# Two residual blocks on one core: attention scores with their masks, and the value products of a head pair, issued as unbroken bundles

## The chip, the core and the metric

One core of a Trainium2 chip runs the whole kernel: TensorE (PE) multiplies matrices into PSUM, VectorE (DVE) and ScalarE (ACT) read PSUM and work in SBUF, GpSimd (POOL) does small pieces, SyncE (SP) issues the transfers. The metric is the device time of one execution in microseconds; lower is better.

## The reference

The input is 256 tokens of 1024 features. Four layers follow each other, each a mixer and a gated feed-forward net. The mixers, cut to what matters here:

```python
# layer 1: stick-breaking attention, 16 heads of 64
z = einsum('bhqd,bhkd->bhqk', q, k) * scale
log_1mb = where(s < t, log_sigmoid(-z), 0)
a = where(s < t, exp(log_sigmoid(z) + cumsum_after(log_1mb)), 0)
o = einsum('bhqk,bhkd->bhqd', a, v)
# layer 2: forgetting attention, 16 heads of 64
cum = cumsum(log_sigmoid(h @ w_fg + b_fg))          # per head and token
logits = where(s <= t, z + cum[t] - cum[s], -inf)
o = einsum('bhqk,bhkd->bhqd', softmax(logits), v)
# layer 3: differential attention, 8 heads with two maps each, over 256 tokens and 256 of a context
p = softmax(einsum("bqmhd,bkmhd->bmhqk", q, k) * scale)
o = einsum("bhqk,bkhd->bqhd", p[:, 0] - lam * p[:, 1], v)
# layer 4: a short convolution
```

Queries are handled in two blocks of 128, so the first block sees 128 keys and the second 256.

## The kernel before

The builder doesn't issue instructions. Each call such as `nc.tensor.matmul` is recorded (`record`) with what it depends on, and when the whole program is recorded, `schedule` makes one order: it walks through a planned time and gives each engine, whenever that engine is free in the plan, the ready operation that was recorded first and whose tiles fit in the buffers. `emit` then issues them in that order; the profile therefore names one line, L544, for nearly every instruction, and work is told apart by tile names. On the chip each engine runs its own list strictly in order.

Matrix products of weights are made in three parts (high times high, high times low, low times high; `mm3`) on float32r. Weights come in chunks of 1 MB (`w`); ScalarE rounds them to `wh` and VectorE takes the difference `wl`. VectorE also does the modulation vectors in the background (`w<-w,rows,vec`, results `raw` and `msh_*`).

In `attention1` (layers 1 and 2) a loop runs over the 8 head pairs: the projection products give `qkps`, copied to `qk`, which holds queries and keys of both heads of a pair, 64 rows each. `scores` makes one PSUM tile `z` per head with two regions: columns 0 to 128 for the first query block, 128 to 384 for the second. Each score product has 64 rows of weights and in float32 it runs as two instructions; the two heads of a pair lie in different halves of the array. Region by region it adds, in layer 2, the gates' sums (a product of a selector column `sel` with `hl`, made in `forget_cum`) and then the mask, a bfloat16 product of the unit matrix with the mask (`bf`). `weights_of` makes the weights `a` on ScalarE and VectorE, `transposed` turns them on TensorE (`atp`) and copies them (`at`), and the value products go to `op`: for each head a 256-column product and a 128-column one, 64 output rows each, so that the two heads again lie in different halves.

In `diff_attention` (layer 3) each of 16 units (head pair, query block, map) has six score products `dz` with 64 rows of weights, three for each head of the pair; then come the softmax (`dmx`, `p`), the transposes `dtp`, the value products `dop`, and the normed result `on`. Products of the values' projection (`acc`) stand between.

At a stage's end the last products go into `acc`; VectorE multiplies these with a gate (`u`), adds them to `x`, and ScalarE, GpSimd and VectorE make the next norm, for which TensorE makes the transposes `tps`.

Of the kernel before, what the change touches and what calls it, by code (L numbers as in the profile page):

```python
# [10 lines left out]
F32 = mybir.dt.float32  # L11
# [252 lines left out]
class Rec:  # L264
# [4 lines left out]
    def __init__(self):  # L269
        self.ops, self.limit, self.count, self.after = [], 0, 0, None  # L270

# [11 lines left out]

    def record(self, eng, fn, args, kw):
# [10 lines left out]
        if fn == "matmul" and not kw["start"]:  # L295
            ins.append(outs[0])
# [86 lines left out]
    def schedule(self, slots):  # L383
# [56 lines left out]
        left, low, far = len(ops), 0, []  # L440
        done = [False] * left
        while left:
# [21 lines left out]
            for e in engines:  # L464
                if engines[e] > now:
                    continue
                while ready[e]:
                    op = heapq.heappop(ready[e])[1]
                    lack = fits(op)
                    if lack is None:  # L470
                        best = op
                        break
                    blocked.setdefault(lack, []).append(op)
                if best:
                    break
# [3 lines left out]
            op = best  # L479
            for t in needs(op):  # L480
                free[t.cls] -= 1
                if t.group:
                    live[t.group] = live.get(t.group, 0) + 1
                t.real = True
                for o in blocked.pop(t.cls, ()):
                    heapq.heappush(pending[o.eng], (now, o.i, o))
# [96 lines left out]
class Builder:  # L583
# [443 lines left out]
    def forget_cum(self):  # L1027

        nc = self.nc
        hl = self.sb.tile([P, S], F32R, tag="hl", name="hl")  # L1030
        sel = self.sb.tile([P, 16], F32R, tag="sel", name="sel")
        nc.vector.tensor_copy(sel, self.cst[:, 256:272])
        zero = self.sb.tile([P, S], F32, tag="hf", name="zero")
# [29 lines left out]
        nc.vector.tensor_copy(hl[0:48], t["d"])  # L1063
        nc.vector.tensor_tensor(out=hl[32:48], in0=t["d"][32:48], in1=hl[32:48].bitcast(F32), op=ALU.subtract)
# [4 lines left out]
    def scores(self, j, qk, stick, cum):  # L1069
# [5 lines left out]
        for t, lo, hi in self.REGIONS:  # L1075
            for hh, z in enumerate(zs):
                rows = slice(64 * hh, 64 * hh + 64)
                q, k = qk[rows, t * P : (t + 1) * P], qk[rows, 256 : 256 + hi - lo]
                nc.tensor.matmul(z[:, lo:hi], lhsT=q, rhs=k, start=True, stop=False)
            for hh, z in enumerate(zs):  # L1080
                if cum is not None:
# [3 lines left out]
                        z[:, lo:hi], lhsT=sel[:, h : h + 1].to_broadcast([P, P]), rhs=hl[:, 0 : hi - lo], start=False,  # L1085
                        stop=False,
                    )
                nc.tensor.matmul(z[:, hi - P : hi], lhsT=self.eye_b, rhs=mask, start=False, stop=True)
# [43 lines left out]
    def attention1(self, i):  # L1132
# [13 lines left out]
        for it in range(KT + 2):  # L1146
# [17 lines left out]
            if 0 <= j < KT:  # L1164
# [3 lines left out]
                for hh in range(2):  # L1168
                    nc.tensor.matmul(
                        op[sl[hh], 0:256], lhsT=vs[0][:, cs[hh]], rhs=ats[hh][:, 0:256], start=True, stop=False  # L1170
                    )
                for hh in range(2):
                    nc.tensor.matmul(
                        op[sl[hh], 128:256], lhsT=vs[1][:, cs[hh]], rhs=ats[hh][:, 256:384], start=False, stop=True
                    )
# [171 lines left out]
    def diff_attention(self):  # L1347
# [67 lines left out]
        for it in range(U + VLAG + 3):  # L1415
# [3 lines left out]
            if it < U:  # L1419
                jp, t, m = it // 4, it % 4 // 2, it % 2  # L1420
                zs = [self.pmm.tile([P, 512], F32, tag="mm", name="dz") for hh in range(2)]
                for a, b in ((0, 0), (0, 1), (1, 0)):
                    for hh in range(2):
                        rows = slice(64 * hh, 64 * hh + 64)
                        nc.tensor.matmul(
                            zs[hh], lhsT=qT[m][a][rows, jp, t * P : (t + 1) * P], rhs=kT[m][jp // 2][b][rows, jp % 2, :],
                            start=a + b == 0, stop=a == 1,
                        )
# [226 lines left out]
```

## Time and profile before

| | |
|---|---|
| median of 3 runs | 1354.19 us (1352.99 to 1358.27) |
| the profiled execution's own time | 1356.83 us |
| its span in the profile | 1355.0 us |
| TensorE busy | 1318.0 us, 97% |
| VectorE busy | 1083.6 us, 80% |
| ScalarE busy | 716.2 us, 53% |
| granted TensorE clock, mean | 0.994 of full speed |

Span is the time from the first to the last instruction. Busy time is the union of an engine's instructions; products overlap in the pipeline, so for TensorE the distance from start to start says more than the length of one. The first attention's loop lies at about 60 to 150 us, the second's at 385 to 470, diff attention's scores at 756 to 846.

### The profile page before, as it was taken

To read this page: it belongs to the slowest core of one execution; us is meant where nothing else is said; L and a number is where in the kernel's file an instruction comes from. 1 tells how busy PE (TensorE), PEld (TensorE's weight loads), DVE (VectorE), ACT (ScalarE), POOL (GpSimd) and SP (SyncE) were. 2 spreads that over 40 slices of the span, in tenths; PEclk is the share of its full clock that TensorE was granted. 3 is DMA by queue.
4 is the path that set the end of the run, shared out by engine and by line. 5 is a ranking of instruction groups with operands and counts; after the bars stand their busy time and mean duration, and the time that the engine had idled before them with its cause. 6 is when DMAs were issued, how large, how long until landed. Compare 5 with 4: busy or idle time off the path is not lost.

```text
span 1355.0 us, 21985 instructions
## 1 busy us (share of the span) xinstructions
PE 1318.0 (97%) x8776; PEld 1178.4 (87%) x8776; DVE 1083.6 (80%) x1825; ACT 716.2 (53%) x1249; POOL 72.4 (5%) x102
## 2 busy tenths in 40 slices
PE   5999899999999999999999999899999999999998
PEld 3788799999898799999988777799999899899997
DVE  6888989899898499999799998886776898855542
ACT  3565655555656484556454567754444545744430
POOL 0000100000100000001033112100000000000000
PEclk9999999999999999999999999899999999999999
DMA  9857578887666256667544641576776688455520
GB/s 360 316 211 272 194 280 321 330 313 293 239 252 252 89 184 260 267 252 270 206 161 173 226 154 63 189 304 254 280 269 260 231 300 309 181 193 186 187 95 32
DMA packets 45320, 311.84 MB, mean 230 GB/s; under 512 B 5280, under 2 KB 5664, under 8 KB 8864
## 3 DMA queue, kind: packets, MB, share of 16 engines
q1 hardware_dynamic: 45216, 310.42, 61.3%
q8 instruction: 69, 1.13, 0.3%
q14 instruction: 35, 0.29, 0.1%
HBM read 309.35 MB, written 1.05 MB: 229 GB/s over the span
## 4 chain that ended last, share of the span: by engine, by line
PE 90%; DVE 6%; ACT 2%; issue 1%; DMA 0%; POOL 0%; SPq 0%; ACTq 0%; POOLq 0%
PE gu L544 34%; PE acc L544 30%; PE qkps L544 7%; PE fp L544 4%; PE cu L544 3%; PE z L544 2%; PE bb L544 2%; PE qps L544 2%; DVE w L544 2%; PE op L544 1%; DVE wl L544 1%; PE dop L544 1%; PE tps L544 1%; PE kc L544 1%; PE atp L544 1%
## 5 line engine op out<-in xcount | busy, mean ns | idle before, releaser
L544 DVE TENSOR_TENSOR wl<-w,wh 128x1024 fp32r<-128x1024 f32 x392 | 470.8, 1220 | 77.9 <-ACT wh L544 54.7
L544 ACT CAST wh<-w 128x1024 fp32r<-128x1024 f32 x392 | 402.4, 1049 | 98.8 <-DMA w<-in_wst_dram 56.7
L544 DVE CUSTOM_DVE_ANT_0 w<-w,rows,vec 128x1024 f32<-128x1024 f32 x192 | 242.4, 1278 | 9.9 <-DMA w<-in_wst_dram 9.6
L544 PE MATMUL gu<-h1h,wh 128*128 128x256 f32 x640 | 181.3, 283 | 0.0
L544 PE MATMUL gu<-h1h,wl 128*128 128x256 f32 x640 | 181.2, 283 | 0.0
L544 PE MATMUL gu<-h0h,wl 128*128 128x256 f32 x640 | 181.1, 283 | 0.0
L544 PE MATMUL gu<-h1l,wh 128*128 128x256 f32 x640 | 181.1, 283 | 0.0
L544 PE MATMUL gu<-h0l,wh 128*128 128x256 f32 x640 | 181.1, 283 | 0.0
L544 PE MATMUL gu<-h0h,wh 128*128 128x256 f32 x640 | 180.9, 283 | 0.0
L544 PE MATMUL acc<-wh,yh 128*128 128x512 f32 x352 | 137.6, 392 | 0.0
L544 PE MATMUL acc<-wl,yh 128*128 128x512 f32 x352 | 137.5, 391 | 0.0
L544 PE MATMUL acc<-wh,yl 128*128 128x512 f32 x352 | 135.3, 389 | 0.0
L544 PEld LDWEIGHTS gu<-h0l,wh 128*128 128x128 f32 x640 | 122.6, 192 | 2.2
L544 PEld LDWEIGHTS gu<-h0h,wh 128*128 128x128 f32 x640 | 122.5, 192 | 2.3
L544 PEld LDWEIGHTS gu<-h1l,wh 128*128 128x128 f32 x640 | 122.8, 192 | 0.1
L544 PEld LDWEIGHTS gu<-h1h,wh 128*128 128x128 f32 x640 | 122.8, 192 | 0.1
L544 PEld LDWEIGHTS gu<-h1h,wl 128*128 128x128 f32 x640 | 122.8, 192 | 0.0
L544 PEld LDWEIGHTS gu<-h0h,wl 128*128 128x128 f32 x640 | 122.6, 192 | 0.0
L544 DVE TENSOR_TENSOR y<-s,gu 128x256 f32<-128x256 f32 x80 | 33.5, 418 | 76.2 <-ACT s L544 76.2
L544 ACT ACTIVATE s<-gu 128x256 f32<-128x256 f32 x40 | 15.4, 385 | 138.0 <-PE gu L544 138.0
L544 PEld LDWEIGHTS acc<-wh,yl 128*128 128x128 f32 x352 | 66.1, 188 | 14.3
L544 PEld LDWEIGHTS acc<-wh,yh 128*128 128x128 f32 x352 | 66.3, 188 | 12.2 <-ACT yh L544 0.2
(364 smaller groups left out, 2690.4 us busy)
## 6 DMA issues: line engine op xcount, KB each, us to landing
w<-in_wst_dram SPq DMA_DIRECT2D x284, 1024.0 KB, 4.9
w<-in_wst_dram SPq DMA_DIRECT2D x16, 512.0 KB, 11.4
x<-in_x_dram SPq DMA_DIRECT2D x2, 512.0 KB, 6.6
cx<-in_ctx_dram SPq DMA_DIRECT2D x2, 512.0 KB, 6.3
out_dram<-x SPq DMA_DIRECT2D x1, 512.0 KB, 2.6
out_dram<-x SPq DMA_DIRECT2D x2, 256.0 KB, 2.0
cst<-in_consts_dram SPq DMA_DIRECT2D x1, 264.0 KB, 5.2
smalls<-in_smalls_dram SPq DMA_DIRECT2D x1, 256.0 KB, 5.2
```

Of the source, the lines that this page charges most:

```text
L544: fn(*[real(a) for a in op.args], **{k: real(v) for k, v in op.kw.items()})
```

## The change

It touches the recording layer and three places that use it.

- `together()` is new: operations recorded inside it form a bundle. The first operation takes over what the others wait for outside the bundle, and their tiles, and `schedule` lets the rest follow it on TensorE before anything else.
- `record` lets an accumulating product depend on its PSUM tile only where earlier writes overlap with it.
- `scores`: the score products of both regions come first (the wide region no longer opens with `start=True`), then, in layer 2, one product of 384 columns per head for the gates' sums in place of one of 128 and one of 256, then all masks.
- `forget_cum`: `hl` has 384 columns, the first 128 repeated, so two copies and two differences are made in place of one each; `hl` and the zero tile now need a slot of the next larger class.
- The four value products of a pair, and the six `dz` products of a unit, are bundles.

```diff
@@ class Rec
+    @contextmanager
+    def together(self):
+
+        n = len(self.ops)
+        yield
+        first, *rest = self.ops[n:]
+        inside = set(self.ops[n:])
+        for op in rest:
+            for d, kind in op.deps.items():
+                if d not in inside:
+                    first.deps.setdefault(d, kind)
+            op.deps.setdefault(first, 1)
+            for t in op.tiles:
+                if t not in first.tiles:
+                    first.tiles.append(t)
+                    t.ops.append(first)
+        self.follow[first] = rest
@@ def record
         if fn == "matmul" and not kw["start"]:
-            ins.append(outs[0])
+            v = outs[0]
+            if any(w[0] & v.mask and w[1] < v.parts[1] and w[2] > v.parts[0] for w in v.t.writes):
+                ins.append(v)
@@ def schedule
+                if e == "PE" and run:
+                    best = run.pop(0)
+                    taken.add(best)
+                    break
                 while ready[e]:
                     op = heapq.heappop(ready[e])[1]
+                    if op in taken:
+                        continue
...
             op = best
+            run += self.follow.get(op, ())
@@ def forget_cum
-        hl = self.sb.tile([P, S], F32R, tag="hl", name="hl")
+        hl = self.sb.tile([P, 384], F32R, tag="hl", name="hl")
...
-        nc.vector.tensor_copy(hl[0:48], t["d"])
-        nc.vector.tensor_tensor(out=hl[32:48], in0=t["d"][32:48], in1=hl[32:48].bitcast(F32), op=ALU.subtract)
+        for lo, n in ((0, P), (P, S)):
+            d, out = t["d"][:, 0:n], hl[:, lo : lo + n]
+            nc.vector.tensor_copy(out[0:48], d)
+            nc.vector.tensor_tensor(out=out[32:48], in0=d[32:48], in1=out[32:48].bitcast(F32), op=ALU.subtract)
@@ def scores
-        for t, lo, hi in self.REGIONS:
-            for hh, z in enumerate(zs):
-                rows = slice(64 * hh, 64 * hh + 64)
-                q, k = qk[rows, t * P : (t + 1) * P], qk[rows, 256 : 256 + hi - lo]
-                nc.tensor.matmul(z[:, lo:hi], lhsT=q, rhs=k, start=True, stop=False)
-            for hh, z in enumerate(zs):
-                if cum is not None:
+        with nc.together():
+            for t, lo, hi in self.REGIONS:
+                for hh, z in enumerate(zs):
+                    rows = slice(64 * hh, 64 * hh + 64)
+                    q, k = qk[rows, t * P : (t + 1) * P], qk[rows, 256 : 256 + hi - lo]
+
+                    nc.tensor.matmul(z[:, lo:hi], lhsT=q, rhs=k, start=t == 0, stop=False)
+            if cum is not None:
+                for hh, z in enumerate(zs):
                     hl, sel = cum
                     h = 2 * j + hh
                     nc.tensor.matmul(
-                        z[:, lo:hi], lhsT=sel[:, h : h + 1].to_broadcast([P, P]), rhs=hl[:, 0 : hi - lo], start=False,
-                        stop=False,
+                        z[:, 0:384], lhsT=sel[:, h : h + 1].to_broadcast([P, P]), rhs=hl, start=False, stop=False
                     )
-                nc.tensor.matmul(z[:, hi - P : hi], lhsT=self.eye_b, rhs=mask, start=False, stop=True)
+            for t, lo, hi in self.REGIONS:
+                for z in zs:
+                    nc.tensor.matmul(z[:, hi - P : hi], lhsT=self.eye_b, rhs=mask, start=False, stop=t == 1)
@@ def attention1, and in the same way the six products of diff_attention
+                with nc.together():
+                    for hh in range(2):
+                        nc.tensor.matmul(
+                            op[sl[hh], 0:256], lhsT=vs[0][:, cs[hh]], rhs=ats[hh][:, 0:256], start=True, stop=False
+                        )
```

What this makes of the order on TensorE is seen at three places; the other engines keep their instructions (VectorE has the two pieces more for `hl`), in an order that is partly changed inside the three attention stages on VectorE and ScalarE, and the order outside of these stages is the same. The first place is TensorE in the second attention's loop, the scores of one head pair (two tiles `z`, one per head; sizes are those of the output). Before:

```order
L544 MATMUL z_4661<-qk_4540 128x128
L544 MATMUL z_4667<-qk_4540 128x128
L544 MATMUL z_4661<-hl_3271,sel_3322 128x128
L544 LDWEIGHTS bf_429
L544 MATMUL z_4661<-bf_429 128x128
L544 MATMUL z_4667<-hl_3271,sel_3322 128x128
L544 LDWEIGHTS bf_429
L544 MATMUL z_4667<-bf_429 128x128
L544 MATMUL z_4661<-qk_4540 128x256
L544 MATMUL z_4667<-qk_4540 128x256
L544 MATMUL z_4661<-hl_3271,sel_3322 128x256
L544 LDWEIGHTS bf_429
```

After the change, the same pair:

```order
L573 MATMUL z_4639<-qk_4503 128x128
L573 MATMUL z_4640<-qk_4503 128x128
L573 MATMUL z_4639<-qk_4503 128x256
L573 MATMUL z_4640<-qk_4503 128x256
L573 MATMUL z_4639<-hl_3271,sel_3322 128x384
L573 MATMUL z_4640<-hl_3271,sel_3322 128x384
L573 LDWEIGHTS bf_429
L573 MATMUL z_4639<-bf_429 128x128
L573 LDWEIGHTS bf_429
L573 MATMUL z_4640<-bf_429 128x128
```

The wide region's score products have moved up behind the narrow ones, the four products for the gates' sums have become two, and the masks stand at the end, four in a row (two more rows of each follow). The second place is TensorE in the same loop, at the value products of the first head pair (`op`; `at` is one head's transposed weights). Before:

```order
L544 MATMUL op_4329<-at_4301,v_736_3897 64x256
L544 MATMUL qkps_4265<-h0h_3757,wh_4062 128x256
L544 MATMUL qkps_4265<-h0l_3767,wh_4062 128x256
L544 MATMUL qkps_4265<-h0h_3757,wl_4098 128x256
L544 MATMUL op_4329<-at_4326,v_736_3897 64x256
L544 MATMUL op_4329<-at_4301,v_737_3982 64x128
L544 MATMUL op_4329<-at_4326,v_737_3982 64x128
```

After the change:

```order
L573 MATMUL qkps_4354<-h0l_3767,wh_4222 128x256
L573 MATMUL op_4363<-at_4327,v_736_3897 64x256
L573 MATMUL op_4363<-at_4352,v_736_3897 64x256
L573 MATMUL op_4363<-at_4327,v_737_3982 64x128
L573 MATMUL op_4363<-at_4352,v_737_3982 64x128
L573 MATMUL qkps_4354<-h0h_3757,wl_4260 128x256
```

The three projection products no longer stand between the heads. In the order before, seven of the sixteen `op` units have other products between their heads, and one between its wide and its narrow products; after, none has. The third place is TensorE in diff attention, one of its last units (`dz`, one tile per head). Before:

```order
L544 MATMUL dz_9161<-kT01h_7784,qT0h_8169 128x512
L544 MATMUL dz_9161<-kT01l_7795,qT0h_8169 128x512
L544 MATMUL dz_9161<-kT01h_7784,qT0l_8187 128x512
L544 MATMUL acc_9084<-wl_8627,doh_8839 128x512
L544 MATMUL dz_9176<-kT01h_7784,qT0h_8169 128x512
L544 MATMUL dz_9176<-kT01l_7795,qT0h_8169 128x512
L544 MATMUL dz_9176<-kT01h_7784,qT0l_8187 128x512
```

After the change:

```order
L573 MATMUL dz_9219<-kT01h_7770,qT0h_8155 128x512
L573 MATMUL dz_9220<-kT01h_7770,qT0h_8155 128x512
L573 MATMUL dz_9219<-kT01l_7781,qT0h_8155 128x512
L573 MATMUL dz_9220<-kT01l_7781,qT0h_8155 128x512
L573 MATMUL dz_9219<-kT01h_7770,qT0l_8173 128x512
L573 MATMUL dz_9220<-kT01h_7770,qT0l_8173 128x512
```

The two heads' products alternate and nothing stands between; in the order before, six of the sixteen units are not in one alternating run.

## Rows read from the trace of the kernel before

**Rows 1.** Windows of the three attention stages; busy us (instructions) of each engine, clock, transfers.

```profile
63.00:136.00 73.00, 72.76 (x540) 58.96 (x539) 64.03 (x119) 42.38 (x79) 0.00 (x0) 1.00 0.67 254
385.00:456.00 71.00, 71.00 (x537) 59.33 (x535) 57.80 (x140) 39.57 (x98) 0.00 (x0) 1.00 0.65 237
756.00:860.00 104.00, 102.31 (x552) 75.68 (x551) 91.31 (x200) 74.64 (x163) 21.36 (x35) 1.00 0.40 146
```

**Rows 2.** Waits of TensorE over the span: total us, times, longest.

```profile
PE tps L544 <- DVE u L544: 4.8, 2, 3.0
...
PE dop L544 <- DVE on L544: 1.3, 3, 0.5
```

**Rows 3.** Timeline of TensorE, first attention: start us, length us, instruction.

```profile
63.02 0.28 PE L544 MATMUL qkps<-h1l,wh 128*128 128x256 f32 x1
63.14 0.28 PE L544 MATMUL qkps<-h1h,wl 128*128 128x256 f32 x1
63.35 0.49 PE L544 MATMUL z<-qk 64*128 64x128 f32 x4
63.77 0.28 PE L544 MATMUL z<-bf 128*128 128x128 bf16 x2
63.99 0.70 PE L544 MATMUL z<-qk 64*128 64x256 f32 x4
64.62 0.28 PE L544 MATMUL z<-bf 128*128 128x128 bf16 x2
```

**Rows 4.** Timeline of TensorE, one score unit of the second attention.

```profile
429.46 0.33 PE L544 MATMUL z<-hl,sel 128*128 128x128 f32 x1
429.62 0.23 PE L544 MATMUL z<-bf 128*128 128x128 bf16 x1
...
429.97 0.70 PE L544 MATMUL z<-qk 64*128 64x256 f32 x4
430.60 0.38 PE L544 MATMUL z<-hl,sel 128*128 128x256 f32 x1
430.83 0.23 PE L544 MATMUL z<-bf 128*128 128x128 bf16 x1
...
431.07 0.23 PE L544 MATMUL z<-bf 128*128 128x128 bf16 x1
```

**Rows 5.** Windows, only instructions with `z`: both stages, one whole unit; no POOL column.

```profile
60.00:160.00 100.00, 13.26 (x96) 5.10 (x64) 0.00 (x0) 13.79 (x32) 1.00 0.63 237
385.00:480.00 95.00, 19.55 (x128) 11.45 (x96) 9.95 (x32) 13.98 (x64) 1.00 0.51 187
429.00:431.60 2.60, 2.27 (x16) 1.36 (x12) 0.00 (x0) 0.00 (x0) 1.00 0.80 255
```

**Rows 6.** Windows, only instructions with `op`: 60:160 and 385:480 summed, then one whole unit.

```profile
sum 195.00, PE 18.63 PEld 8.92 DVE 6.58 ACT 6.23; mean PE 9.31 PEld 4.46 DVE 3.29 ACT 3.11
...
432.00:434.50 2.50, 0.87 (x8) 0.49 (x8) 0.00 (x0) 0.14 (x1) 1.00 0.41 167
```

**Rows 7.** Windows, only instructions with `dz`: all units, a whole one, a broken one.

```profile
756.00:846.00 90.00, 19.77 (x96) 9.55 (x96) 20.79 (x32) 27.50 (x64) 1.00 0.36 130
771.50:773.00 1.50, 0.97 (x6) 0.48 (x6) 0.00 (x0) 1.17 (x3) 1.00 0.21 87
831.00:834.00 3.00, 1.92 (x6) 0.96 (x6) 1.75 (x3) 1.71 (x4) 1.00 0.72 300
```

**Rows 8.** Windows of diff attention, four of 10 us from 766 to 806, their sum.

```profile
sum 40.00, PE 38.83 PEld 27.97 DVE 39.27 ACT 28.27 POOL 4.22; mean PE 9.71 PEld 6.99 DVE 9.82 ACT 7.07 POOL 1.06
```

**Rows 9.** Timeline of VectorE at the end of diff attention.

```profile
860.56 1.22 DVE L544 TENSOR_TENSOR wl<-w,wh 128x1024 fp32r<-128x1024 f32 x1
861.69 1.29 DVE L544 TENSOR_TENSOR u<-acc,rows 128x512 f32<-128x512 f32 x2
```

**Rows 10.** Timeline of VectorE at the end of the first attention.

```profile
144.04 0.08 DVE L544 DVE_READ_ACCUMULATOR2_ANT raw<- 128x1 f32 x1
145.71 0.16 DVE L544 SCALAR_TENSOR_TENSOR sst<-ss 128x1 f32<-128x1 f32 x1 [1.59 <-ACT junk L544]
```

More of the change, by code (lines that the diff above doesn't have):

```diff
@@ L1 @@
 import math
-from contextlib import ExitStack
+from contextlib import ExitStack, contextmanager
 import numpy as np
@@ L270, in __init__ @@
         self.ops, self.limit, self.count, self.after = [], 0, 0, None
+        self.follow = {}
     def __getattr__(self, name):
@@ L440, in schedule @@
         left, low, far = len(ops), 0, []
+        run, taken = [], set()
         done = [False] * left
@@ L1029, in forget_cum @@
         nc = self.nc
-        hl = self.sb.tile([P, S], F32R, tag="hl", name="hl")
+        hl = self.sb.tile([P, 384], F32R, tag="hl", name="hl")
         sel = self.sb.tile([P, 16], F32R, tag="sel", name="sel")
         nc.vector.tensor_copy(sel, self.cst[:, 256:272])
-        zero = self.sb.tile([P, S], F32, tag="hf", name="zero")
+        zero = self.sb.tile([P, 384], F32, tag="hf", name="zero")
         nc.gpsimd.memset(zero, 0.0)
@@ L1167, in attention1 @@
                 cs = [slice((2 * j + hh) * 64, (2 * j + hh) * 64 + 64) for hh in range(2)]
[L1168 to L1175, printed above, removed]
+                with nc.together():
[3 more added lines that the diff above has]
+                        )
+                    for hh in range(2):
+                        nc.tensor.matmul(
+                            op[sl[hh], 128:256], lhsT=vs[1][:, cs[hh]], rhs=ats[hh][:, 256:384], start=False, stop=True
+                        )
                 os_[j] = self.split(op[:, 0:256], S, "o")
@@ L1421, in diff_attention @@
                 zs = [self.pmm.tile([P, 512], F32, tag="mm", name="dz") for hh in range(2)]
[L1422 to L1428, printed above, removed]
+                with nc.together():
+                    for a, b in ((0, 0), (0, 1), (1, 0)):
+                        for hh in range(2):
+                            rows = slice(64 * hh, 64 * hh + 64)
+                            nc.tensor.matmul(
+                                zs[hh], lhsT=qT[m][a][rows, jp, t * P : (t + 1) * P],
+                                rhs=kT[m][jp // 2][b][rows, jp % 2, :], start=a + b == 0, stop=a == 1,
+                            )
                 if m == 0:
```

## The prediction

> **What bounds the kernel now.** I read the three attention stages first, in the view by windows, because the diff touches nothing else [rows 1]. The reader is to see that TensorE is busy for 72.76 of 73 us, 71.00 of 71 and 102.31 of 104: it has work nearly all the time, at full granted clock. VectorE is second, with 64.03, 57.80 and 91.31. The view of waits then says where TensorE does stand idle: at stage ends, for the sums that go into the next norm (`u`, 4.8 us in two waits, the longest 3.0) [rows 2]; in the middle of the stages the largest is 1.3 in three waits, for `on`. So what the stages' TensorE work loses in length should come off the end, as far as VectorE follows. Next I read the timeline of one score unit, to see how long each piece holds TensorE, measured from start to start, since products overlap [rows 3, 4]; and last the busy time of each bundle's own instructions, which shows at once which units are in pieces [rows 5 to 7].
>
> **What a break costs.** A product with 64 rows of weights for one head runs beside that of the other head: the four instructions of the narrow region take 0.42 us together and the four of the wide one 0.63 [rows 3]. A piece that stands alone has no partner, so it takes as long as the pair would. A diff-attention unit in one piece is busy for 0.97; one whose two heads stand apart for 1.92, twice as much [rows 7]. Besides, TensorE pays on the way in: a whole-array product follows its like after 0.12, but the first half-array product after 0.21 [rows 3]. I take the same for the way back, 0.18 for a trip, an estimate from those rows.
>
> **Value products** (`op`). Sixteen units are busy for 18.63 in sum, a whole one for 0.87 [rows 6]. Sixteen whole ones would be 13.9, so 4.7 is lost to breaks: by the old order seven units have their heads apart and one its halves. Eight trips of 0.18 add up to 1.4, but the tail of a piece also lies over the next product; between 4.7 (no trips) and 6.1 I take 5.5.
>
> **Diff attention's scores** (`dz`). Sixteen units are busy for 19.77 against 16 x 0.97 = 15.5 [rows 7], so 4.25 is lost; the order shows six units that aren't in one alternating run, with six ways out and back among them, 1.1. I take 5.3, with 4.2 below (trips free) and 5.5 above (a trip more).
>
> **Scores of the two first attentions** (`z`). In the first one a unit is whole for 1.55 (63.35 to 64.62, and 0.28) [rows 3]. The change lets the wide region follow the narrow one at once, which takes out the 0.22 between the first mask and the wide region, and puts two more masks at the end; a second mask follows the first after 0.28 - 0.23 = 0.05 or 0.06 [rows 3, 4], so 0.12 comes back and 0.10 is saved. Eight units of 1.45 are 11.6 where 13.26 were busy [rows 5]: 1.65, which holds the one unit that was mixed up.
>
> In the second attention 0.51 lies between the end of the narrow region and the wide one (429.46 to 429.97: two products for the gates' sums and two masks), and 0.47 from the wide region's end to the last mask (430.60 to 431.07) [rows 4]. After the change there is one product per head of 384 columns, and then four masks. No row has 384 columns. A gates' product of 128 holds TensorE for 0.16 until its mask, one of 256 for 0.23 [rows 4], so 0.07 for 128 more columns and 0.30 for 384. That holds for the second product, which a mask follows. The first is followed by its like: from below 0.12 + 0.07 = 0.19 (as whole-array products follow each other [rows 3]), from above 0.30. I take 0.19, since what follows is of the same kind and type. With three more mask steps that is 0.67 in place of 0.98: 0.31 saved, 0.20 at the upper bound. Eight units of 2.27 - 0.31 = 1.96 are 15.7 where 19.55 were busy [rows 5]: 3.9, and 3.0 at the upper bound. Two or three trips fewer in both attentions: 0.4. Together 5.9 for `z`, from 4.5 to 6.3.
>
> A rule of the Trainium skill speaks against the 0.19: "TensorE: Matmul & The Clock Gate", Part 3, says that a weight load overlaps products in flight only where it goes to other row groups. By it the second 384 product would start only after its load, 0.11 later in each of eight units, and the sum would be 0.9 less. The trace doesn't bear it out for whole-array products that follow at 0.12 [rows 3].
>
> **The gates' prologue** gets two copies and two differences of 48x256 and 48x128 in place of one each. They lie on VectorE ahead of the first score unit of that layer, where TensorE has projection products to do; I cost them at nothing; if that cover is gone, the two more cost between 0.16 (the shortest VectorE instruction shown [rows 10]) and 0.65 (one 512 wide, half of the two at 861.69 [rows 9]) each, 0.3 to 1.3 once. No transfer is added or moved: SyncE's order is the same row for row. The waits that a bundle adds are costed with the rivals.
>
> **The sum.** 5.5 + 5.3 + 5.9 = 16.7 us of TensorE's work, 13.4 to 17.9. By stage: 4.4 in the first attention, 7.0 in the second, 5.3 in diff attention.
>
> **What of it reaches the end.** In the second attention all: VectorE has 13 us to spare [rows 1]. In the first, VectorE ends its last background product at 144.12 and then waits 1.59 for the sums of squares [rows 10]. Beyond that 1.6, TensorE's gain counts only if VectorE comes earlier too; it has 9 us of idle time in the stage [rows 1], part of it waiting for TensorE's results, so I let 3.0 of 4.4 through. In diff attention VectorE works for 39.27 of 40 us from 766 to 806 [rows 8]: the two of the six broken units that lie up to there (1.8 of the 5.3, taking them alike) give nothing back. At the stage's end VectorE is still splitting weights at 860.56 and comes to `u` at 861.69 without a pause [rows 9], while TensorE waits 3.0 for `u` [rows 2]. Of the other 3.5 I let 2.7 through, because the later units' normalizations on VectorE come earlier with TensorE. 3.0 + 7.0 + 2.7 = 12.7.
>
> The profiled execution took 1356.83, with a span of 1355.0; the median shown is 1354.19, 2.6 below it. Its counterpart after the change would be a span of 1342.3, and the median 1341.5.
>
> **Rivals.**
> 1. *All of it counts*: VectorE's lateness is itself made by TensorE's late scores. For it: of VectorE's 12.7 us without work in the diff stage only 0.73 lie between 766 and 806 [rows 1, 8], so later on it waits for TensorE. Against it: the stage's end [rows 9]. 1354.2 - 16.7 = 1337.5.
> 2. *VectorE is the bound in two stages*: the first attention gives its 1.6 and diff attention nothing. 1354.2 - 8.6 = 1345.6. For it: [rows 8 to 10]; against it: VectorE's idle time in the first stage [rows 1].
> 3. *The first 384 product holds TensorE as long as the one before a mask*, 0.30 in place of 0.19, in the eight units of the second attention: 12.7 - 0.9 = 11.8, so 1342.4. The step of 0.12 between whole-array products speaks against it [rows 3]. It is what the skill's rule on weight loads, cited above, would make of the time.
> 4. *The bundles don't help*: what stood between the pieces was there because a piece's operand was late, and TensorE now waits at the bundle's head in its place. Then 1354, within half a per cent. Against it: between the halves of one diff unit stood a single product, so its partner's operands were ready.
> 5. *Slower*: a bundle is 4 to 10 products of which the first waits for the operands of all, both transposed heads or both free score buffers, and everything on TensorE is queued behind it; the normalizations on VectorE and ScalarE wait for the scores in turn. There are 48 bundles. From 16.7 / 48 = 0.35 us of waiting at each the gain is gone; for 0.5% slower (6.8 us) it takes 0.49 at each. The size isn't absurd, since the old order found three projection products' time between the heads of an `op` unit; but in the new one such products stand ahead of the bundle, and TensorE has next to no wait in mid-stage now [rows 2]. At 0.5 each it would be 1361.5.
>
> **How the numbers follow.** Forecast (12.7, 1341.5) 0.50, with 1338 to 1345 as its own range; all of it 0.20; VectorE as the bound 0.17; the longer 384 product 0.04; no help 0.05; slower 0.04. The range starts at the upper sum and a fast run, 1353.0 - 17.9 = 1335.1, and reaches to VectorE as the bound with the lower values of the second attention (6.1 in place of 7.0) and 1.4 more for waits at bundles (0.03 each), 1348. Half a per cent, 6.8 us, is about what a measurement tells from no change here, so faster means below 1347.4: 0.50 + 0.20 + 0.04 and most of 0.17 make 0.88; same 0.09; slower 0.03.
>
> **What the profile will show.** Right, if sixteen `op` units are busy for about 14 us, `dz` for 15.5, `z` for 11.6 and 15.7, and a 384 product is followed by the other after about 0.19; and if TensorE's wait for `u` after diff attention grows by part of the 2.6 that I leave out in that stage. Wrong, if TensorE gets waits of its own in mid-stage for `at`, `qk` or free score buffers, if `u` starts no earlier than now after its stage's start, or if the feed-forward stages, whose order isn't changed, give time back.

## The result and the profile after

The changed kernel takes 1337.88 us in the median of 4 runs (1337.31 to 1338.73), the kernel before 1354.26 on the same chip (1352.99 to 1358.27): ratio 0.9875, 95% interval 0.9853 to 0.9896, 16.4 us less. The forecast was 1341.5, the range 1335 to 1348; the time lies by the rival "all of it counts" (1337.5). The profiled execution's span is 1335.9 us, with 1301.9 of TensorE busy and 1082.9 of VectorE. That is 19.1 less than the profiled execution of before, but 2.1 of it lies ahead of the first projection product (`qkps` starts at 49.64 after 51.75), where the change does nothing. Between the three attention stages (203.98 us, and 183.8) and behind them (485.1 before, 485.2 now) nothing has moved.

Windows of the changed kernel, only instructions with `z` (two rows), with `op` (the sum of both stages), with `dz`; they answer to [rows 5 to 7]:

```profile
60.00:160.00 100.00, 10.04 (x96) 4.19 (x64) 0.00 (x0) 14.09 (x32) 0.98 0.67 247
380.00:480.00 100.00, 13.68 (x112) 6.56 (x80) 9.91 (x32) 14.18 (x64) 1.00 0.53 199
sum 200.00, PE 13.93 PEld 7.76 DVE 6.63 ACT 6.22; mean PE 6.97 PEld 3.88 DVE 3.31 ACT 3.11
...
740.00:846.00 106.00, 16.28 (x96) 8.35 (x96) 20.64 (x32) 26.94 (x64) 1.00 0.42 156
```

`op` came out at 13.9 as expected, `dz` at 16.3 (expected 15.5), `z` at 10.0 and 13.7 where 11.6 and 15.7 were expected: the scores gained far more than the prediction gave them. The timeline of one score unit of each attention shows where; "PEld" is the weight loader, and a number in brackets is its idle time:

```profile
61.24 0.93 PE L573 MATMUL z<-qk 64*128 64x128 f32 x8
62.10 0.40 PE L573 MATMUL z<-bf 128*128 128x128 bf16 x4
62.31 0.36 PE L573 MATMUL qkps<-h0h,wh 128*128 128x256 f32 x1
...
414.53 0.52 PEld L573 LDWEIGHTS z<-qk 64*128 64x128 f32 x8
414.54 0.93 PE L573 MATMUL z<-qk 64*128 64x128 f32 x8
415.39 0.30 PEld L573 LDWEIGHTS z<-hl,sel 128*128 128x128 f32 x2 [0.33 <-issue]
415.39 0.61 PE L573 MATMUL z<-hl,sel 128*128 128x384 f32 x2
415.84 0.23 PEld L573 LDWEIGHTS <-bf 128*128 128x128 bf16 x4 [0.16 <-issue]
415.85 0.40 PE L573 MATMUL z<-bf 128*128 128x128 bf16 x4
416.08 0.39 PE L573 MATMUL atp<-eye,a 128*128 128x128 f32 x2
```

Three lines of the trace of before go with them: the operation after the unit of [rows 3], and the start of the unit of [rows 4] and what follows it.

```profile
64.72 0.37 PE L544 MATMUL qkps<-h0h,wh 128*128 128x256 f32 x1
...
429.04 0.49 PE L544 MATMUL z<-qk 64*128 64x128 f32 x4
...
431.14 0.82 PE L544 MATMUL atp<-eye,a 128*128 128x128 f32 x6
```

From its first product to the next operation a unit now takes 1.07 us (61.24 to 62.31) where it took 1.37 (63.35 to 64.72), and 1.55 (414.53 to 416.08) where it took 2.10 (429.04 to 431.14). The eight score instructions hold TensorE for 0.86 together; before they took 0.42 + 0.63 with masks between [rows 3]. So the score products themselves have become 0.19 shorter in each unit. Product by product, half of that lies at the narrow region's last product, followed after 0.10 in place of 0.20, and half at the wide region's first, 0.21 in place of 0.31: its loads now run under the narrow region's products.

The waits of TensorE over the span answer to [rows 2]:

```profile
PE tps L573 <- DVE u L573: 5.0, 2, 3.5
...
PE dop L573 <- DVE on L573: 1.3, 3, 0.8
```

The longest wait for `u`, after diff attention, has grown from 3.0 to 3.5. VectorE at the end of the first attention (two rows) and of diff attention (two), with TensorE's first transposes behind it, answers to [rows 9, 10]:

```profile
137.74 0.08 DVE L573 DVE_READ_ACCUMULATOR2_ANT raw<- 128x1 f32 x1
138.37 0.16 DVE L573 SCALAR_TENSOR_TENSOR sst<-ss 128x1 f32<-128x1 f32 x1 [0.54 <-ACT junk L573]
...
841.48 1.22 DVE L573 TENSOR_TENSOR wl<-w,wh 128x1024 fp32r<-128x1024 f32 x1
842.62 1.28 DVE L573 TENSOR_TENSOR u<-acc,rows 128x512 f32<-128x512 f32 x2
...
847.95 1.97 PE L573 MATMUL tps<-eye,u 128*128 128x128 f32 x8 [3.47 <-DVE u L573]
```

In the first attention VectorE ends its background work 6.3 us earlier than before (137.74 after 144.04), 4.2 earlier against the stage's start (first `qkps` at 49.64 after 51.75), and still waits 0.54. So it seems to have been held up by TensorE, and came along. In diff attention it goes from splitting weights to `u` without a pause, as before.

For the terms of the sum, busy time is a poor measure, since it counts a piece's tail that lies over the next product. Summed instead are the distances from one product's start to the next one's over the whole timeline, with the waits that it shows taken off (us):

```
tile                      before    changed    difference   predicted
z,  first attention        12.05       8.97       -3.08  }
z,  second attention       18.19      12.50       -5.69  }    -5.9
op, both                   16.96      12.82       -4.14  }
acc beside op, both        48.07      46.61       -1.46  }    -5.5
dz                         18.25      15.24       -3.01       -5.3
sum                                              -17.38      -16.7
```

### The profile page after: what moved, and what is told of

The parts are those of the page before. It is cut to its first block, busy times and chain, and to the rows that moved or that the text cites. A ratio compares the mean times of both kernels' runs of the same rounds, so it can differ in the third digit from the quotient of the medians.

```text
span 1335.9 us, 21951 instructions
## 1 busy us (share of the span) xinstructions
PE 1301.9 (97%) x8760; PEld 1172.1 (88%) x8760; DVE 1082.9 (81%) x1827; ACT 715.1 (54%) x1249; POOL 76.1 (6%) x102
## 4 chain that ended last, share of the span: by engine, by line
PE 85%; DVE 6%; ACT 3%; issue 2%; DMA 1%; POOL 1%; SPq 0%; ACTq 0%; POOLq 0%; DVEq 0%
PE gu L573 34%; PE acc L573 28%; PE qkps L573 6%; PE fp L573 4%; PE cu L573 3%; DVE w L573 2%; PE bb L573 2%; PE qps L573 2%; PE z L573 2%; PE tps L573 1%; DMA w<-in_wst_dram 1%; PE op L573 1%; DVE wl L573 1%; PE kc L573 1%; PE atp L573 1%
```

## The experiments

All change the changed kernel. Stage lengths are read from each run's timeline: from the first `qkps` to the first `gu` for the first two attentions, from the first `kc` to the first `fp` for diff attention (`gu` and `fp` are products of the feed-forward net behind, `kc` those of the context's keys). What lies ahead of the first `qkps` took 49.6 to 52.0 us from execution to execution, whatever the kernel; the first attention, with the same order, 113.0 to 114.5; the second 107.64 to 107.67. So a difference in the second attention can be read to a tenth, in the first only to about one. Most of what varies in the first is TensorE's granted clock at the stage's end, as windows of the changed kernel, of its second execution and of run 2 show (the seventh figure, behind POOL's, is the clock):

```profile
140.00:163.00 23.00, 19.72 (x127) 17.29 (x127) 21.93 (x39) 17.63 (x36) 3.75 (x4) 0.93 0.51 179
...
140.00:162.00 22.00, 17.71 (x122) 15.20 (x121) 20.93 (x38) 17.42 (x35) 3.75 (x4) 1.00 0.49 171
...
140.00:167.00 27.00, 23.13 (x135) 20.62 (x134) 24.20 (x43) 19.61 (x39) 4.30 (x5) 0.87 0.51 180
```

Each 0.07 below 1.00 is a stretch of 3.4 us at the lower level, 1.2 in place of 2.4 GHz, behind waits of TensorE for `u` and the next norm, which all these executions have. Of those with the same order, the three without a stretch (changed again, two gates' products, no maxima) took 113.0, those with one at 147 us 113.0 to 113.6, those with one at 159 (`dz` in pairs, mask between) 114.4 and 114.5.

The runs come from other chips than the result. The kernel before took 1355.3 to 1356.1 there in the median, the changed kernel 1337.78, so a difference of medians holds to about 1 us.

| kernel | median us | first att. | second att. | diff att. |
|---|---|---|---|---|
| before | 1354.26 | 120.26 | 116.73 | 193.37 |
| changed | 1337.88 | 113.63 | 107.67 | 191.96 |
| changed again | 1337.78 | 113.01 | 107.66 | 192.57 |
| `dz` loose | 1340.29 | 113.47 | 107.65 | 193.93 |
| `op` loose | 1342.83 | 117.67 | 111.57 | 191.51 |
| `z` by region | 1345.53 | 116.25 | 112.71 | 191.56 |
| two gates' products | 1341.22 | 112.99 | 110.67 | 191.97 |
| `z` loose | 1340.98 | 116.53 | 109.84 | 191.98 |
| `op`, `z` joined | 1338.05 | 114.00 | 106.75 | 191.92 |
| `dz` in pairs | 1346.91 | 114.44 | 107.65 | 201.78 |
| `dz` head by head | 1337.37 | 112.99 | 107.64 | 191.53 |
| `dz`, mask between | 1348.40 | 114.47 | 107.66 | 201.38 |
| no maxima | 1331.18 | 113.00 | 107.67 | 186.57 |
| joined, ScalarE | 1343.12 | 114.01 | 106.75 | 198.89 |

Theory after the result: TensorE's switches between whole-array and half-array products, and half-array products without a partner, are what the change saves, and nearly all of it arrives in the first two attentions; in diff attention VectorE's lateness takes a part. Rivals: the bundles as such pay, or the two gates' products, or VectorE bounds diff attention altogether.

**1. The `dz` bundle undone.**

```diff
-                with nc.together():
-                    for a, b in ((0, 0), (0, 1), (1, 0)):
+                for a, b in ((0, 0), (0, 1), (1, 0)):
```

> The changed kernel with the six `dz` products of a unit recorded without a bundle; the other parts stay. The order has 22 runs of `dz` products in place of 15, as before the change. Theory (steps): the distances from start to start say that the `dz` bundles took 3.0 us off TensorE and that 2.1 of it arrived, so 1340.0 us (1339.2 to 1341). By the prediction's term 5.3 us of TensorE and 2.7 arriving: 1340.6, so here the profile must tell: start-to-start of `dz` 18.3 us by the steps, over 20 by the prediction. Rival (VectorE is the bound in diff attention): 1337.9, no change.

Measured: 1340.29 (1339.73 to 1342.83), ratio to before 0.9892 (0.9877 to 0.9906). From start to start the `dz` products take 18.24 us, 3.0 more. So the bundle is worth 3.0 in these products, not 5.3, and about 2 in time. The order in this stage is that of before, and so is the stage's length (193.93 and 193.37).

**2. The `op` bundle undone**, in the same way.

> The changed kernel with the value products `op` recorded without a bundle; the other parts stay. The order has nine of sixteen units with their heads apart. Theory: the prediction's term was right, 5.5 us for eight units, 6.2 for nine, and nearly all of it arrives since TensorE is the bound in both stages: 1343.8 us (1342.8 to 1344.5). Rival (only the second attention counts, VectorE holds the first): about half, 1341.

Measured: 1342.83 (1342.03 to 1347.7), ratio 0.9912 (0.9896 to 0.9928): 5.0 more, at the lower end. `op` and the `acc` products beside it take 6.1 us more from start to start, as the term said. The second attention alone is 3.9 longer. The first is 3.2 to 4.7 longer in the profile, of which `op` and `acc` make 2.4 and the clock at the end, shown above, a part; the median leaves 1.1 for it. So the first counts too, but how much is open.

**3. Region by region, inside an unbroken bundle.**

```diff
+                    nc.tensor.matmul(z[:, lo:hi], lhsT=q, rhs=k, start=True, stop=False)
+                for hh, z in enumerate(zs):
+                    if cum is not None:
...
+                            z[:, lo:hi], lhsT=sel[:, h : h + 1].to_broadcast([P, P]), rhs=hl[:, lo:hi], start=False,
...
+                    nc.tensor.matmul(z[:, hi - P : hi], lhsT=self.eye_b, rhs=mask, start=False, stop=True)
```

> The changed kernel with each `z` unit still an unbroken bundle, but inside it region by region as before the change: narrow scores, gates' sums of 128 columns, masks, wide scores, gates' sums of 256 columns, masks. Theory (loader): a trip through whole-array products inside a unit costs about 0.2 us at the loader besides the products themselves; whole units were 0.33 us (first attention) and 0.55 (second) longer before the change, so 8 x 0.88 = 7.0 us: 1344.9 us (1344 to 1346). Prediction's terms: 8 x (0.10 + 0.31) = 3.3 us: 1341.2. Rival (the bundle itself, not the order inside, is what pays): under 1339.

Measured: 1345.53 (1343.13 to 1345.93), ratio 0.9923 (0.9909 to 0.9937): 7.7 more, with 6.9 more from start to start in `z`. The order inside the unit pays, far more than the prediction's 3.3. Of the 6.9, 2.4 are the first attention's, 0.30 for each of eight units; in the second, 0.9 is the gates' four products in place of two, by run 4, so the order alone makes 6.0. Timeline of one unit of this run, TensorE and loader:

```profile
422.06 0.49 PE L573 MATMUL z<-qk 64*128 64x128 f32 x4
422.48 0.33 PE L573 MATMUL z<-hl,sel 128*128 128x128 f32 x1
...
423.00 0.70 PE L573 MATMUL z<-qk 64*128 64x256 f32 x4
423.63 0.18 PEld L573 LDWEIGHTS z<-hl,sel 128*128 128x128 f32 x1 [0.33 <-issue]
```

Narrow region 0.42 and wide one 0.63 again, in place of 0.86 together, and the way out and in for a second time. The Trainium skill, "TensorEngine Tiling (Array Packing)", Key Properties, says that changing the tiling mode drains TensorE; the loader's 0.33 us of idle time ahead of the first whole-array load agrees.

**4. Two gates' products per head.**

```diff
-                        z[:, 0:384], lhsT=sel[:, h : h + 1].to_broadcast([P, P]), rhs=hl, start=False, stop=False
+                            z[:, lo:hi], lhsT=sel[:, h : h + 1].to_broadcast([P, P]), rhs=hl[:, lo:hi], start=False,
```

> The changed kernel with the order inside a `z` unit as changed, but the gates' sums as a product of 128 and one of 256 columns per head in place of one of 384. Theory (loader): the pair of 384 products now takes 0.46 us from start to start; four products that follow their like after 0.12 and one switch of 0.1 would take 0.58, so 8 x 0.12 = 1.0 us: 1338.9 us (1338 to 1339.5). Rival (the prediction's weighing, by which the second attention's 0.31 us per unit comes from having two gates' products in place of four): 8 x 0.31 = 2.5 us: 1340.4.

Measured: 1341.22 (1340.43 to 1342.01), ratio 0.9895 (0.9882 to 0.9908): 3.4 more, above both. The gates' products cost 0.86 more from start to start, as the theory said. The rest is new: the order in the second attention has moved in other places too, and TensorE waits there, where the changed kernel has no such wait:

```profile
PE qkps L573 <- ACT at L573: 1.1, 1, 1.1
...
PE qkps L573 <- ACT e L573: 0.5, 1, 0.5
```

So the 384-column product is worth 0.9 by itself; the time of this run measures a shifted order as well.

**5. The changed kernel again.**

> The changed kernel itself once more, on the chip of the other runs of this call, so that they can be set against it. Expected 1337.9 us, 1337 to 1340 with another chip.

Measured: 1337.78 (1337.59 to 1339.96), ratio 0.9871 (0.9855 to 0.9887).

**6. Value products joined to scores.**

```diff
+                with nc.together():
+                    if j >= 2:
+                        op = self.value_products(j - 2, vs, atd.pop(j - 2))
+                    zs = self.scores(j, qk[j], stick, cum)
```

> A version that may beat both: the value products of a pair wait one pass of the loop more and stand in one bundle ahead of the scores of the pair two further on (twelve of sixteen units; the last two of a stage stay alone). Theory (loader): each way from whole-array products to half-array ones or back costs 0.1 us; if products on column halves pass into products on row halves without such a wait, 12 x 0.2 = 2.4 us less than the changed kernel; if that is a switch too, 12 x 0.1 = 1.2 less. Rival: the bundle's head now waits for more (one more PSUM tile, the scores' operands), new waits on TensorE in mid-stage, no gain or slower by up to 3.

Measured: 1338.05 (1335.97 to 1338.72), ratio 0.9864 (0.9846 to 0.9883): not told apart from the changed kernel. The second attention is 0.9 shorter, 0.15 for each of six units, between the two estimates. That `op` into `z` is a switch too, as the smaller one had it, shows in the timeline of this run:

```profile
91.28 0.87 PE L573 MATMUL op<-at,v 128*64 128x256 f32 x8
92.08 0.52 PEld L573 LDWEIGHTS z<-qk 64*128 64x128 f32 x8 [0.17 <-issue]
```

The loader still waits 0.17 between column halves and row halves, and the last `op` product is followed after 0.20, where its like follows after 0.10. In the first attention nothing is settled.

**7. Both maps in one bundle.**

```diff
+                    pair = [[self.pmm.tile([P, 512], F32, tag="mm", name="dz") for hh in range(2)] for _ in range(2)]
+                    with nc.together():
+                        for mm in range(2):
```

> A version that may beat both: the `dz` products of both maps, two units, as one bundle of twelve, eight bundles in place of sixteen. In the changed kernel two units that happened to stand next to each other took 1.95 us together, single ones 1.04 to 1.10 each. Theory (TensorE bounds diff attention too): 7 x 0.2 = 1.4 us less on TensorE, 1.0 less in time. Rival (VectorE bounds diff attention): no change. Second rival: four score tiles at once leave too few PSUM tiles for the transposes and value products, so TensorE waits in mid-stage and it is 2 us slower or more.

Measured: 1346.91 (1344.83 to 1350.64), ratio 0.9938 (0.9921 to 0.9955): 9.1 slower. The `dz` products do fall by 2.4 more from start to start (12.80), but TensorE waits:

```profile
PE dop L573 <- DVE on L573: 4.2, 5, 1.6
...
PE dtp L573 <- ACT p L573: 3.6, 2, 3.3
...
PE dop L573 <- ACT p L573: 2.3, 3, 1.0
```

The second rival's outcome. Whether too few PSUM tiles or the coarser order makes these waits wasn't told apart. The granted clock, too, was 0.51 from 839.0 to 842.4, behind the wait of 3.3, and 0.50 from 852.8 to 856.0.

**8. `dz` head by head.**

```diff
-                    for a, b in ((0, 0), (0, 1), (1, 0)):
-                        for hh in range(2):
+                    for hh in range(2):
+                        for a, b in ((0, 0), (0, 1), (1, 0)):
```

> The changed kernel with each `dz` bundle written head by head: three products of the first head, then three of the second, so that partners no longer stand next to each other. It measures the price of a broken unit and what of it arrives. By the steps of a lone piece (0.23 us from product to product) a unit takes five steps of 0.23 and a way back in place of two steps: 0.69 us more each, 11.0 on TensorE. Theory (some 70% of TensorE's time in diff attention arrives): 7.7 us slower than the changed kernel, 6 to 11. Prediction's premise (half alone takes as long as the pair, 0.95 more per unit): 15.2 on TensorE, over 10 arriving. Rival (VectorE is the bound and hides it): under 4.

Measured: 1337.37 (1335.88 to 1338.59), ratio 0.9864 (0.9848 to 0.988): no cost at all, against every expectation. In the timeline the products still go two by two, one of each head:

```profile
752.74 0.19 PEld L573 LDWEIGHTS dz<-kT00h,qT0h 64*128 64x128 f32 x2 [0.35 <-issue]
752.75 0.50 PE L573 MATMUL dz<-kT00h,qT0h 64*128 64x512 f32 x2
753.08 0.40 PE L573 MATMUL dz<-kT00l,qT0h 64*128 64x512 f32 x2
753.32 0.40 PE L573 MATMUL dz<-kT00h,qT0l 64*128 64x512 f32 x2
```

So alternation isn't needed here, where nothing of the whole array stands between. The second head's first product starts 0.010 us after the first head's in 14 of the 16 units; in the changed kernel, where it is next in the list, it is 0.003 to 0.004 wherever it has no wait of its own.

**9. A whole-array product between the heads.**

```diff
+                    for hh in range(2):
+                        if hh:
+                            nc.tensor.matmul(zs[1][:, 0:P], lhsT=self.eye_b, rhs=self.causal_b, start=True, stop=True)
```

> The changed kernel with each `dz` bundle head by head and one whole-array product of 128 columns (a mask product whose result the next product overwrites) between the heads. It mends the run before it, in which three products of one head followed by three of the other still went in pairs. By the trace of before, where a piece of three up to the next whole-array product took 0.89 us, a unit now takes 0.89 + 0.15 + 0.89 in place of 0.90: 1.03 us more each, 16.5 on TensorE. Theory (some 70% of TensorE's time in diff attention arrives, as 2.1 of 3.05 did): 11.5 us slower than the changed kernel, 1349.4 us (1347 to 1352). Rival (VectorE is the bound there and hides it): under 4 us, below 1342. Second rival (TensorE alone is the bound): 16 us, over 1352.5.

Measured: 1348.40 (1347.95 to 1351.39), ratio 0.9952 (0.9939 to 0.9964): 10.6 more than the changed kernel. One unit in its timeline:

```profile
752.50 0.49 PE L573 MATMUL dz<-kT10h,qT1h 64*128 64x512 f32 x1
...
753.39 0.23 PE L573 MATMUL dz<-bf 128*128 128x128 bf16 x1
753.55 0.49 PE L573 MATMUL dz<-kT10h,qT1h 64*128 64x512 f32 x1
...
754.44 0.50 PE L573 MATMUL acc<-wh,hc1h 128*128 128x512 f32 x1
```

A unit cut in two takes 1.94 us (752.50 to 754.44) in place of 0.90. All sixteen take 15.0 more from start to start, the mask products included; the stage grows by 8.8 to 9.4, the time by 10.6. A part of what is missing went into waits of TensorE that were there already: that for `u` after the stage is 1.7 in place of 3.5, that for `on` 0.7 in place of 1.3. Another 2.6 is less from start to start in `acc` and `dop`. Not hidden, and not all of it either.

**10. VectorE relieved.**

```diff
-                    nc.vector.tensor_reduce(out=mx, in_=z, axis=AX.X, op=ALU.max)
-                    nc.vector.scalar_tensor_tensor(out=nb, in0=mx, scalar=-1.0, in1=r, op0=ALU.mult, op1=ALU.mult)
```

> The changed kernel without the row maxima of diff attention and their scaling (32 of 0.68 and 32 of 0.15 us on VectorE: 26.5 us less), and with logits made 1000 times smaller so that the exponentials stay finite; this part of the computation is left out. Theory (VectorE's lateness costs diff attention what did not arrive of the `dz` bundles' gain: 0.9 us of waits in the middle and at the end, and more that was lost before the change as well): TensorE's waits in the stage fall from 6.4 to about 4, the time by 2 to 3 us below the changed kernel, 1335.3 us. Rival (TensorE alone is the bound): under 0.5 us, 1337.5. Second rival (VectorE is the bound through the whole stage): more than 6 us.

Measured: 1331.18 (1330.49 to 1332.53), ratio 0.982 (0.9807 to 0.9833): 6.6 less, at the second rival's bound, with no TensorE work taken out. The wait for `u` after the stage is 2.1; TensorE's gaps there fall from 6.4 to 3.9, and the products beside VectorE's results (`dop`, `dz`, `acc`) take another 3.0 less from start to start; small delays that the view of waits doesn't list and the order, which moved, aren't told apart there. The stage is 5.0 to 6.0 shorter, so what VectorE does there costs it more than the theory said. The maxima also stood in the chain from the scores to the exponentials: whether their time on VectorE or their place in that chain counts, this run doesn't tell.

**11. The new order of `z` without its bundle.**

> The changed kernel with the order inside a `z` unit as changed but without its bundle. The order has 20 runs of `z` products in place of 16: two units of the second attention are in pieces and two masks stand apart. Theory (a unit's order pays by itself, the bundle only for the few units that would fall apart; each extra run costs about 0.2 us for the way out and in, a lone piece up to 0.4 more): 4 runs make 0.8 to 2.4 us, 1339.4 us. Rival (the bundle is what pays): over 1342.

Measured: 1340.98 (1340.61 to 1341.89), ratio 0.9892 (0.9878 to 0.9905): 3.2 more, above the theory and near the rival. In the second attention two units have their heads apart and one its scores apart from the gates' products; in the first, one unit is in three pieces. The second attention is 2.2 longer, 1.7 of it in `z` from start to start and 0.4 in a new wait for `e`, which stands between two such heads. The first is 2.1 longer than in the executions whose clock fell as late in the stage (runs 7 and 9): 0.3 in `z`, 1.1 in waits, the largest part for `at` (0.8 after 0.2), the rest small. So the bundle is worth having besides the order.

**12. Joined, and a VectorE step moved to ScalarE.**

```diff
-                        nc.vector.tensor_scalar(out=p[0], in0=p[0], scalar1=rs[:, 0:1], scalar2=None, op0=ALU.mult)
+                        nc.scalar.activation(out=p[0], in_=p[0], func=AF.Copy, scale=rs[:, 0:1])
```

> A version that may beat both: value products joined to the scores as in the run before, and in diff attention the scaling of the first map by its sum (16 of 0.48 us) moved from VectorE to ScalarE. Theory: 0.9 us from each of the two first attentions (the second one's length fell so when they were joined), and 7.6 us less work on VectorE, whose lateness at the end of diff attention costs TensorE up to 1.9 us: 1 to 2 more. 1335.0 us (1334 to 1337). Rival (ScalarE, busy for 70 to 85% of that stage, becomes late in its place with the exponentials and the rounding of weights): 1337 or slower.

Measured: 1343.12 (1342.15 to 1345.1), ratio 0.9908 (0.9895 to 0.9922). The second attention is 0.9 shorter once more (106.75), but diff attention 6 to 7 longer. TensorE waits for what comes out of the moved step, and the granted clock is down around these waits, 0.50 from 835.5 to 845.5 (the changed kernel's was 1.00 from 835 to 846):

```profile
PE dtp L573 <- DVE p L573: 2.9, 1, 2.9
...
PE rowps L573 <- ACT p L573: 1.4, 1, 1.4
...
835.50:845.50 10.00, 6.64 (x28) 5.75 (x28) 8.33 (x14) 7.87 (x15) 0.79 (x2) 0.50 0.75 286
```

How much of the 6 to 7 us is the waits and how much the clock wasn't told apart.

No version tried is measurably faster than the changed kernel with the whole computation.

## Why the prediction was right, and which terms were off

The mechanism was right: TensorE bounds the stages, breaks cost it time, and what it loses in length mostly comes off the end. That the sum came out (16.7, measured 17.4) is luck: two errors of size went opposite ways, 2.9 too little for `z` and 2.3 too much for `dz` (1.1 too much with what lies beside `dz`, below). The time lies in the range, but at rival 1's figure and not at the forecast: 16.4 arrived where 12.7 was let through.

*Value products, 5.5*: measured 5.6 (4.14 in `op` and 1.46 in the `acc` products behind the pieces); undoing the bundle gave 6.1 for nine units.

*Scores, 5.9*: measured 8.8. The step that failed is the unit that was whole before: "takes out the 0.22 between the first mask and the wide region", 0.10 saved per unit in the first attention, 0.31 in the second. Measured are 0.30 and 0.55. The masks and gates' products gave about what was said, 0.11 and 0.36; what was left out is that the score products get shorter too, 0.42 + 0.63 before and 0.86 now, 0.19 in each of sixteen units, 3.1 in all. Of the trip through whole-array products only the way back into the wide region was in the prediction; the way out behind the narrow region and the wide region's first load were not. Run 3 measured the whole trip: 0.30 us per unit in the first attention.

*The 384-column products*: 0.19 and 0.30 predicted, 0.28 (first) and 0.18 (second, until the mask) by their start times. The sum was right, 0.46 against 0.49; the roles were reversed. The first one costs more because it is the first after half-array products. So the rival's 0.30 for it was nearly right, and the loss of 0.9 that the rival put to it didn't come. The rule cited from the Trainium skill, "TensorE: Matmul & The Clock Gate", Part 3, on loads under products in flight gives nearly that first step, 0.30; but the trace has both loads done by 415.69, while the first product runs to 415.83, so the second load did run under it.

*The gates' prologue, nothing*: right. VectorE's two more pieces take 0.5 and the last is done at 382.5, ahead of the first product that reads them (385.6).

*Diff scores, 5.3*: measured 3.0 in the `dz` products. The 4.25 was mis-sized in two ways. It was busy time, which counts the tails of pieces over other products: from start to start the units of before took 18.25 against 16 x 0.90, 3.85 more. And two bundles of the changed kernel took 1.38 in place of 0.90: the bundle orders the plan, but on the chip each product keeps its own wait. In this timeline of the changed kernel the second head's load waits, and the first head's product stands alone:

```profile
766.81 0.99 PE L573 MATMUL dz<-kT10h,qT1h 64*128 64x512 f32 x2
...
767.29 0.18 PEld L573 LDWEIGHTS dz<-kT10h,qT1h 64*128 64x128 f32 x1 [0.30 <-DVE on L573]
```

The 1.1 for ways out and back is there, though not in the table: beyond the median distance of their kind, the products just ahead of and behind a run of `dz` took 4.2 us before (22 runs) and take 3.0 now (15 runs). The sum over all products beside `dz` hides it, because others of them, ahead of short delays that the view of waits doesn't list, take 1.5 more.

*What arrives*: 3.0 of 4.4, 7.0 of 7.0 and 2.7 of 5.3 predicted. In the first attention all of 5.6 to within what an execution varies: VectorE came earlier with TensorE, the prediction's rival 1. In the second all: 9.1. In diff attention 0.8 to 2, out of 3.0 in `dz` and 1.2 beside it. The wait for `u` grew as forecast, but only by 0.5 (0.8 in the second execution); the rest went into the short delays. Runs 9 and 10 show that both engines hold that stage: 15.0 more on TensorE give 10.6, 26.5 less on VectorE give 6.6.

*No help, slower*: nothing of it showed in the changed kernel. TensorE waits 0.9 for `at` once in the first attention (0.2 before, and 0.2 in the second execution) and in sum as long as before for `on`, 1.3 in three waits, the longest now 0.8 in place of 0.5. Run 7 shows what a larger bundle would have done.

## What to carry to other kernels

Count switches between whole-array and half-array products inside a unit too, not only where a unit is in pieces: a trip through whole-array products inside a score unit cost 0.30 us here, and putting the half-array products of a unit next to each other was worth 6.0 us on TensorE, as much as any other part. Measure TensorE's terms from start to start, and look at the neighbours one by one: a sum over them can hide a gain behind short delays. Before a part of a planned order is undone or enlarged, expect the plan to move elsewhere (0.9 us of work made 3.4 us of time in run 4).

## What the runs showed that was not expected

Three half-array products of one head written ahead of three of the other ran in pairs, 0.01 us apart (run 8), though the list is said above to run strictly in order. Whether the chip or the building of the program brings them together isn't shown; that the distance is three times that of partners who follow each other in the list (0.003 to 0.004) would fit a chip that reads the list in order and lets each half go ahead by itself. The first float32 product of the whole array after half-array ones takes 0.10 us longer than its like: 0.28 against 0.18 for 384 columns, with the loader idle for 0.33 ahead of it, 0.22 against 0.12 for 256, 0.34 against 0.23 for 512. For a bfloat16 mask it is 0.01 (0.067 against 0.056).
